# A decoder trunk on one core: value products of two heads at a time, four heads as one run

## The chip, the cores and the metric

One core of a Trainium2 chip runs the whole program. The metric is the device time of one launch in microseconds (us); the figure for a kernel is the median of its runs. The engines are TensorE (PE in the profile; PEld is its loading of weights), VectorE (DVE), ScalarE (ACT), GpSimd (POOL) and SyncE (SP, which here only issues transfers).

## The reference

Two decoder layers over 1024 tokens of width 1024, in fp32. Layer 0, which the change touches, is attention with two families of eight heads of 64 columns each. Layer 1 is a recurrent layer. Each layer ends with a gated embedding. For a block of 128 queries:

```
# NSA heads (2 groups of 4 heads share keys and values)
p_c = softmax(q . compressed keys + bias);   o_c = p_c @ compressed values
imp = per group, sum of p_c over heads and over the blocks that overlap
sel = top 8 of the 64-key blocks by imp (first, current and previous forced)
o_s = softmax(q . k over selected blocks + bias) @ v_s
o_w = softmax(q . k over the last 512 keys + bias) @ v_w
o_a = g0 * o_c + g1 * o_s + g2 * o_w
# DSA heads (all 8 share one key and value head)
sel = top 256 keys by an indexer's score
o_b = softmax(q . k over selected keys + bias) @ v
y = concat(o_a * silu(a_z), o_b * silu(b_z)) @ w_out
```

The compressed keys and values come from windows of 32 tokens (stride 16) through a small two-layer network with a tanh-formed SiLU (`cmp_w1`, `cmp_w2`).

## The kernel before

**Ahead of attention.** Weights are projected one 128-column chunk at a time (`proj`, L197): 48 products of 512 columns, as each operand is split into a high and a low part. Beside the projections VectorE finds, for each query block t of 2 to 7, the threshold of the top 256 keys (`search_step`), and then `choose(t)` (L475) turns scores into a mask `mall`. The last two blocks, 4 and 3, are chosen after the projection that makes the compressed keys' input (L606 to L609). `blocks_of(w, ps)` (L548) then scales the projected keys (w = 0) or values (w = 1) into `kc2`, copies them shifted by one token, and adds the position terms into two tiles `blk`. `compress(w)` (L572) multiplies these by four loaded parts `w1` (products `ps_hid`), and goes over a tanh, a transposition (`ps_hidt`) and a second product (`ps_cmp`). `first_keys` projects the first half of the window and the selected-block keys (`ps_kw`). The scratch tiles `tk`, `kc2`, `blk`, `w1` and others share seven buffers of the pool `big`.

**Attention** (`attention`, L815) goes over 16 blocks: eight query blocks t, each for the two groups p. Each block has 12 heads or units: four window heads, four DSA heads, four selected-block heads, all with the queries on the output partitions of the scores. Unit j passes three stages:

- `scores` (L633): products `ps_s` of up to 512 columns into PSUM, bias or mask and a running minimum on VectorE (L653), exponential with its sum on ScalarE (L657), division and gate on VectorE or GpSimd (L662). The result is `L`, with one row per query.
- four units later `transposed` (L665): TensorE transposes each 128 keys of `L` into the PSUM tile `ps_pt`, ScalarE copies that into `pt`.
- six units later `weighted` (L678), for two units at a time: for each key tile one product for the first head and one for the second, each with 64 columns of values as weights and 128 queries as moving columns. The head's number decides which half of the 128 output partitions of `ps_o` is written.

`begin` (L796) opens the accumulation in `ps_o` with the compressed branch, and `finish` (L802) multiplies it by the gate path into `y`. There is one PSUM bank for `ps_o`, three for `ps_s`, three for `ps_pt` and one (tag "c") for the compressed branch's scores `ps_c` and transposes `ps_ct`. During unit 5 of a block, `prepare` (L756) works out the compressed branch of the next block with `compressed` (L689). `projections` (L823) weaves the second halves of the window and selected keys (`ps_fill`) into the first blocks.

**What sets the order.** A scheduler orders each engine's instructions by data and priority when the program is built; instructions issued through `PV`, `PA` and `PG` (class `Pinned`) keep the order in which the program gives them. On the chip each engine goes through its list in that order and waits where an input isn't there.

Of the kernel before, what the change touches and what calls it, by code (L numbers as in the profile page):

```python
# [25 lines left out]
STEPS = (2, 3)  # L26
WARM = 14
LOAD, PREP = 1, 5
# [30 lines left out]
def trunk_kernel(ctx: ExitStack, tc: tile.TileContext, a, out):  # L59
# [318 lines left out]
    A.activation(biasc[:, :, 48:63], ps[:, :240].rearrange("p (j h) -> p h j", h=16)[:, :8], AF.Copy)  # L378
# [169 lines left out]
    def blocks_of(w, ps):  # L548
        src = []
        for g in range(2):  # L550
            own = slice(g * 64, g * 64 + 64)
            k2 = big(name="kc2")
            V.tensor_tensor(k2[lo], ps[own], nrow[own], OP.mult)
            A.activation(k2[hi, :1023], k2[lo, 1:], AF.Copy)
            src.append(k2)
        for q in range(2):
            bt = big(name="blk")
            b = bt.rearrange("p (l g c) -> p l g c", l=8, g=2)
            V.memset(b[:, :, :, 63:], 0.0)
            for g in range(2):  # L560
                k2 = src[g][:]
                win = bass.AP(tensor=k2.tensor, offset=k2.offset + q * 16, ap=[k2.ap[0], [2, 8], [16, 63]])
                V.tensor_tensor(b[:, :, g, :63], win,
# [69 lines left out]
    def scores(t, g, h, q, keys, k0, far, near, scale, vi):  # L633
# [8 lines left out]
        for c, m in zip(cut, np.diff(cut).tolist()):  # L642
            s = psum.tile([128, 512], F32, name="ps_s", tag="s", bufs=3)
# [21 lines left out]
    def transposed(L, t, k0):  # L665
        nk = t + 1 - k0 // 128
        ps = []
        for b in range(0, nk, 4):
# [7 lines left out]
        return ps  # L676

    def weighted(pair, O, last):  # L678

        nk = len(pair[0][0])  # L680
        for i in range(nk):
            for ps, d in pair:
                h, vi = d["h"], d["vi"]
                c = h // 2 + (2 if vi == 4 else 0)
                T.matmul(O[(h % 2) * 64:(h % 2) * 64 + 64, c * 128:c * 128 + 128],  # L685
                         tok[:, d["k0"] // 128 + i, vi * 64:vi * 64 + 64], ps[i],
                         start=False, stop=last and i == nk - 1, skip_group_check=True)

    def compressed(g, t, q):  # L689
        s = psum.tile([128, 512], F32, name="ps_c", tag="c", bufs=1)  # L690
        for h in range(4):
            for i in range(2):
                T.matmul(s[:, h * 64:(h + 1) * 64], q[:, i, h, :], kcs[:, g * 64:(g + 1) * 64],
                         start=i == 0, stop=i == 1)
# [33 lines left out]
        pt = psum.tile([128, 512], F32, name="ps_ct", tag="c", bufs=1)  # L728
# [4 lines left out]
        return p, sel  # L733
# [22 lines left out]
    def prepare(u):  # L756
# [35 lines left out]
        u.heads = win[:2] + dsa[:2] + win[2:] + dsa[2:] + chosen  # L792
# [3 lines left out]
    def begin(u):  # L796
        u.O = psum.tile([128, 512], F32, name="ps_o", tag="o", bufs=1)
        T.matmul(u.O[:, :256], vc2[:, u.p], u.cmp, start=True, stop=False, skip_group_check=True)
# [16 lines left out]
    def attention():  # L815
# [4 lines left out]
        prepare(blocks[0])  # L820
        units = [(u, k) for u in range(len(order)) for k in range(12)]
# [33 lines left out]
        for j in range(len(units) + AHEAD):  # L855
            for _ in range(FILL[min(j, len(FILL) - 1)]):
                next(fill, None)
            if j < len(units):
# [5 lines left out]
                if k == PREP and i + 1 < len(order):  # L864
                    prepare(blocks[i + 1])
            b = j - AHEAD + MID
            if 0 <= b < len(units):
                i, k = units[b]
                d = blocks[i].heads[k]
                pend[b] = transposed(pend[b], d["t"], d["k0"])  # L870
# [13 lines left out]
    first = attention()  # L884
    leave("ps1", "att", "l0")
# [422 lines left out]
def _layout(i):  # L1308
# [10 lines left out]
    cols = lambda s, n: w[:, s:s + n]  # L1319
    o["wa"] = chunks(np.concatenate([cols(2456, 256), cols(2712, 64), cols(2328, 64), cols(512, 256), cols(768, 128),  # L1320
# [43 lines left out]
```

## Time and profile before

| | us |
|---|---|
| median of 3 runs | 1541.84 (1539.64 to 1543.18) |
| the profiled execution | 1540.62 |
| its span, first to last instruction | 1538.8 |
| attention, first to last `y` | 361.5 (373.6 to 735.1) |
| TensorE busy in the span | 1482.5 |
| VectorE busy | 997.8 |
| ScalarE busy | 799.6 |

The profile is of one execution. Busy time is the union of an engine's instructions, so matmuls that overlap count once, and a matmul's record includes its way through the array after its last column has entered. An idle stretch is put down to what released the engine. The granted clock is given as a share of 2.4 GHz. An fp32 product appears as two records in the trace (1632 records of value products for 816 in the program).

### The profile page before, as it was taken

How to read it: one execution, taken by the hardware profiler on the slowest of the kernel's cores; microseconds unless marked ns; L12 is line 12 of the kernel's file. 1: busy time of each engine (PE TensorE's matmuls, PEld its weight loads, DVE VectorE, ACT ScalarE, POOL GpSimd, SP SyncE). 2: the span in 40 equal slices, each digit the busy share in tenths (PEclk: the TensorE clock that was granted, in tenths of full speed). 3: DMA queues.
4: the chain of work that ended last, by engine and by line, in shares of the span. 5: the costliest groups of instructions: out<-in, count | busy, mean ns of one | idle time of the engine just before them, and what ended most of it. 6: DMA issues, size and time to landing. Idle time of an engine off the chain costs nothing.

```text
span 1538.8 us, 24004 instructions
## 1 busy us (share of the span) xinstructions
PE 1482.5 (96%) x8622; PEld 1223.3 (79%) x8622; DVE 997.8 (65%) x2465; ACT 799.6 (52%) x1667; POOL 509.6 (33%) x506
## 2 busy tenths in 40 slices
PE   9989999987999999999999999999999999999995
PEld 7867887876677888888888889887778888788785
DVE  6378888956789988886234464277776744434446
ACT  6466887225778788777223335366664422223311
POOL 3223443312344443443233412032220123233726
PEclk9999999998999999999999999999999999999997
DMA  4402442354322211200332322011110021222203
GB/s 179 124 28 83 137 138 97 127 176 111 99 69 70 56 49 36 56 22 1 124 103 89 117 76 75 14 49 48 41 40 17 28 83 48 76 85 86 76 1 110
DMA packets 78087, 117.23 MB, mean 76 GB/s; under 512 B 7615, under 2 KB 43072, under 8 KB 77968
## 3 DMA queue, kind: packets, MB, share of 16 engines
q1 hardware_dynamic: 71360, 99.42, 21.1%
q0 software_dynamic: 3952, 12.62, 2.4%
q10 hardware_dynamic: 2656, 3.66, 0.9%
q8 instruction: 68, 1.11, 0.3%
q14 instruction: 51, 0.42, 0.1%
HBM read 94.83 MB, written 24.13 MB: 77 GB/s over the span
## 4 chain that ended last, share of the span: by engine, by line
PE 67%; DVE 15%; ACT 9%; issue 5%; POOL 3%; DMA 2%; SPq 0%; DVEq 0%; POOLq 0%; ACTq 0%
PE ps_proj L194 10%; PE ps_proj L193 10%; PE ps_proj L195 10%; ACT junka L54 5%; PE ps_o L685 5%; PE ps_s L645 5%; PE ps_pt L672 4%; PE ps_gate L193 3%; DVE L L653 3%; PE ps_gate L194 3%; PE ps_gate L195 3%; DVE tk L54 2%; DVE qz L54 1%; DVE junk L54 1%; PE ps_hid L579 1%
## 5 line engine op out<-in xcount | busy, mean ns | idle before, releaser
L121 POOL TENSOR_TENSOR wl<-w,wh 128x512 fp32r<-128x512 f32 (+1 forms) x104 | 152.2, 1482 | 434.7 <-ACT wh L120 434.2
L120 ACT ACTIVATE wh<-w 128x512 fp32r<-128x512 f32 (+1 forms) x104 | 61.1, 621 | 224.3 <-PE ps_proj L194 182.3
L657 ACT ACTIVATE L<-L,st 128x640 f32<-128x640 f32 (+7 forms) x192 | 143.1, 746 | 33.7 <-DVE st L653 26.0
L193 PE MATMUL ps_proj<-x1n,wh 128*128 128x512 f32 x384 | 152.4, 397 | 0.0
L195 PE MATMUL ps_proj<-x1n,wl 128*128 128x512 f32 x384 | 151.8, 395 | 0.0
L194 PE MATMUL ps_proj<-x1n,wh 128*128 128x512 f32 x384 | 151.5, 394 | 0.0
L645 PE MATMUL ps_s<-key,q 128*128 128x256 f32 (+3 forms) x576 | 150.3, 368 | 1.0 <-DVE st L653 0.6
L674 ACT ACTIVATE pt<-ps_pt 128x512 f32<-128x512 f32 (+3 forms) x288 | 124.3, 464 | 37.5 <-PE ps_pt L672 27.5
L193 PE MATMUL ps_proj<-x,wh 128*128 128x512 f32 x336 | 133.1, 396 | 0.4 <-DVE qz L54 0.3
L195 PE MATMUL ps_proj<-x,wl 128*128 128x512 f32 x336 | 133.0, 396 | 0.0
L194 PE MATMUL ps_proj<-x,wh 128*128 128x512 f32 x336 | 132.5, 394 | 0.0
L672 PE MATMUL ps_pt<-cst,L 128*128 128x128 f32 x816 | 125.0, 276 | 5.5 <-DVE L L662 4.3
L685 PE MATMUL ps_o<-pt,tok 128*64 128x128 f32 x1632 | 121.8, 281 | 0.7 <-ACT pt L674 0.7
L54 POOL TENSOR_TENSOR wl<-w,wh 128x512 fp32r<-128x512 f32 x46 | 62.4, 1361 | 169.8 <-ACT wh L54 167.1
L645 PEld LDWEIGHTS ps_s<-key,q 128*128 128x128 f32 x576 | 94.7, 193 | 24.2 <-issue 10.2
L672 PEld LDWEIGHTS ps_pt<-cst,L 128*128 128x128 f32 x816 | 95.2, 141 | 18.6 <-issue 5.5
L685 PEld LDWEIGHTS ps_o<-pt,tok 128*64 128x64 f32 x1632 | 91.7, 137 | 22.5 <-issue 18.4
L54 ACT ACTIVATE junka<-xall,cand 128x384 int8<-128x384 f32 (+2 forms) x93 | 83.6, 899 | 29.2 <-DVE cand L54 27.1
L194 PE MATMUL ps_proj<-y,wh 128*128 128x512 f32 x240 | 93.5, 390 | 0.8 <-DVE y L121 0.8
L193 PE MATMUL ps_proj<-y,wh 128*128 128x512 f32 x240 | 93.5, 390 | 0.1
L195 PE MATMUL ps_proj<-y,wl 128*128 128x512 f32 x240 | 93.4, 389 | 0.0
L54 DVE TENSOR_SCALAR_CACHE_REDUCE junk<-xall,cand 128x512 bf16<-128x512 f32 (+2 forms) x93 | 85.9, 924 | 3.3
(430 smaller groups left out, 3623.7 us busy)
## 6 DMA issues: line engine op xcount, KB each, us to landing
q<-qd SPq DMA_DIRECT2D x64, 256.0 KB, 4.0
w<-in_ra_dram SPq DMA_DIRECT2D x48, 256.0 KB, 2.7
w<-in_wa_dram POOLq DMA_DIRECT2D x46, 256.0 KB, 3.1
qd<-qst SPq DMA_DIRECT2D x32, 256.0 KB, 3.2
w<-in_wo_dram SPq DMA_DIRECT2D x32, 256.0 KB, 2.7
w<-in_gatew_dram SPq DMA_DIRECT2D x32, 256.0 KB, 2.8
x<-in_x_dram SPq DMA_DIRECT2D x8, 512.0 KB, 8.8
zd<-qz SPq DMA_DIRECT2D x8, 512.0 KB, 2.6
```

The costliest lines, as they stand in the source:

```text
L54: return self.tc.keep_in_program_order(getattr(self.eng, name)(*args, **kw))
L120: A.activation(h, src, AF.Copy)
L121: eng.tensor_tensor(l, src, rd(h), op=OP.subtract)
L193: T.matmul(ps, wh, xh, start=first, stop=False)
L194: T.matmul(ps, wh, xl, start=False, stop=False)
L195: T.matmul(ps, wl, xh, start=False, stop=last)
L645: T.matmul(s[:, :m], q[:, i, h, :], keys[:, k0 + c:k0 + c + m], start=i == 0, stop=i == 1)
L653: V.tensor_tensor_reduce(view(L[:, x:y]), view(s[:, x - c:y - c]), pen, 1.0, prev, OP.add, OP.min, st[:, k:k + 1])
L657: A.activation(L[:, :n], L[:, :n], AF.Exp, bias=prev, scale=-1.0, accum_out=st[:, 2:3])
L672: T.transpose(pt[:, i * 128:(i + 1) * 128], L[:, (b + i) * 128:(b + i + 1) * 128], ident)
L674: A.activation(p[:, :m * 128], pt[:, :m * 128], AF.Copy)
L685: T.matmul(O[(h % 2) * 64:(h % 2) * 64 + 64, c * 128:c * 128 + 128], tok[:, d["k0"] // 128 + i, vi * 64:vi * 64 + 64], ps[i], start=False, ...
```

## The change

It does five things:

- `transposed` puts two heads (k and k + 1) into one tile `pt` of 128 x 2 x 512, and `weighted` takes four heads at once: for each key tile two products, each of 64 value columns by 256 moving columns (two heads), the first into the upper half of the output partitions, the second into the lower. They run when the fourth head's turn has come, with a raised priority (`BURST`), and `begin` stands directly ahead of the first of them.
- The twelve heads of a block go in the order window, DSA, selected, four each (before: two window, two DSA, two window, two DSA, four selected). So that heads 0 and 1 lie in one half and 2 and 3 in the other, the compressed branch, the gate columns, the gate paths and the output weights are permuted, on the host or by a bias copy in four pieces.
- The compressed branch's scores use the bank ring of `ps_s`, which has four banks instead of three; its transposes use that of `ps_pt`. Tag "c" is gone.
- `compressed` is cut in two: its transposes (`compressed_rows`) come at unit 10 of the block instead of unit 5.
- `blocks_of` for keys and values comes ahead of the `choose` of block 4 and of block 3, and its VectorE and ScalarE instructions are pinned.

```diff
-    for t in ends[0]:
-        choose(t)
     blocks_of(0, ps)
+    choose(ends[0][0])
     ps = proj(None, X, w=got[17][0])
     wks = prefetch(5)
+    blocks_of(1, ps)
     compress(0)
-    blocks_of(1, ps)
+    choose(ends[0][1])
     first_keys(wkw, kw)
...
-            s = psum.tile([128, 512], F32, name="ps_s", tag="s", bufs=3)
+            s = psum.tile([128, 512], F32, name="ps_s", tag="s", bufs=4)
...
-            p = small.tile([128, 512], F32, name="pt", bufs=PT)
-            A.activation(p[:, :m * 128], pt[:, :m * 128], AF.Copy)
-            ps += [p[:, i * 128:(i + 1) * 128] for i in range(m)]
+            p = first["pt"][b // 4] if j else small.tile([128, 2, 512], F32, name="pt", bufs=PT)
+            A.activation(p[:, j, :m * 128], pt[:, :m * 128], AF.Copy)
+            d["pt"].append(p)
...
-        for i in range(nk):
-            for ps, d in pair:
-                h, vi = d["h"], d["vi"]
-                c = h // 2 + (2 if vi == 4 else 0)
-                T.matmul(O[(h % 2) * 64:(h % 2) * 64 + 64, c * 128:c * 128 + 128],
-                         tok[:, d["k0"] // 128 + i, vi * 64:vi * 64 + 64], ps[i],
-                         start=False, stop=last and i == nk - 1, skip_group_check=True)
+        for i in reversed(range(nk)):
+            for r in (1, 0):
+                T.matmul(O[r * 64:r * 64 + 64, c:c + 256], tok[:, d["k0"] // 128 + i, vi * 64:vi * 64 + 64],
+                         quad[2 * r]["pt"][i // 4][:, :, i % 4 * 128:i % 4 * 128 + 128],
+                         start=False, stop=last and i == 0, skip_group_check=True)
...
-        s = psum.tile([128, 512], F32, name="ps_c", tag="c", bufs=1)
+        s = psum.tile([128, 512], F32, name="ps_c", tag="s", bufs=4)
...
-        pt = psum.tile([128, 512], F32, name="ps_ct", tag="c", bufs=1)
+        return pc, sel
+
+    def compressed_rows(pc):
+        pt = psum.tile([128, 512], F32, name="ps_ct", tag="pt", bufs=3)
...
-        u.heads = win[:2] + dsa[:2] + win[2:] + dsa[2:] + chosen
+        u.heads = win + dsa + chosen
...
-                if k == 0:
-                    begin(u)
-                if k % 2:
-                    weighted([(pend.pop(c - 1), u.heads[k - 1]), (pend.pop(c), u.heads[k])], u.O, k == 11)
+                if k % 4 == 3:
+                    with tc.high_priority(offset=BURST):
+                        if k == 3:
+                            begin(u)
+                        weighted(u.heads[k - 3:k + 1], u.O, k == 11)
```

What this does to the order on TensorE is seen at three places. The first is in the middle of attention, at query block 5, before the change (`ps_s` are scores, `ps_pt` transposes, `ps_o` value products; x10 is ten in a row):

```order
L672 MATMUL ps_pt<-cst,L 128x128 x5
L685 MATMUL ps_o<-pt,tok 64x128 x10
L645 MATMUL ps_s<-key,q 128x384 x2
L645 MATMUL ps_s<-key,q 128x256 x2
L672 MATMUL ps_pt<-cst,L 128x128 x5
L645 MATMUL ps_s<-key,q 128x384 x2
L645 MATMUL ps_s<-key,q 128x256 x2
L672 MATMUL ps_pt<-cst,L 128x128 x5
L685 MATMUL ps_o<-pt,tok 64x128 x10
L645 MATMUL ps_s<-key,q 128x384 x2
```

On the same engine, in the same part of the program, after the change:

```order
L647 MATMUL ps_s<-key,q 128x256 x2
L676 MATMUL ps_pt<-cst,L 128x128 x5
L647 MATMUL ps_s<-key,q 128x384 x2
L647 MATMUL ps_s<-key,q 128x256 x2
L676 MATMUL ps_pt<-cst,L 128x128 x5
L647 MATMUL ps_s<-key,q 128x384 x2
L647 MATMUL ps_s<-key,q 128x256 x2
L676 MATMUL ps_pt<-cst,L 128x128 x4
L688 MATMUL ps_o<-pt,tok 64x256 x10
L676 MATMUL ps_pt<-cst,L 128x128
L647 MATMUL ps_s<-key,q 128x384 x2
L647 MATMUL ps_s<-key,q 128x256 x2
```

A run of value products came after every second head and comes after every fourth, with as many products of twice the width. Over the whole program 123 runs with 816 products became 48 with 408; of the 123, 44 had an odd count.

The second place is on TensorE at the end of the projections, before the change (`ps_proj` is the last projection, `ps_hid` the first compressing product, `ps_kw` the window keys):

```order
L194 MATMUL ps_proj<-x_109,wh 128x512
L195 MATMUL ps_proj<-x_109,wl 128x512
L579 MATMUL ps_hid<-w_2608,blk 128x256 x4
L579 MATMUL ps_hid<-w_2614,blk 128x256 x4
L579 MATMUL ps_hid<-w_2620,blk 128x256 x4
L579 MATMUL ps_hid<-w_2626,blk 128x256 x4
L193 MATMUL ps_kw<-x_102,wh 128x512
```

And on TensorE around the same four groups of `ps_hid` after the change:

```order
L195 MATMUL ps_kw<-x_103,wh 128x512
L196 MATMUL ps_kw<-x_103,wl 128x512
L194 MATMUL ps_kw<-x_103,wh 128x512
L581 MATMUL ps_hid<-w_2615,blk 128x256 x4
L581 MATMUL ps_hid<-w_2621,blk 128x256 x4
L581 MATMUL ps_hid<-w_2627,blk 128x256 x4
L581 MATMUL ps_hid<-w_2633,blk 128x256 x4
L195 MATMUL ps_kw<-x_103,wh 128x512
```

`ps_hid` followed the last projection directly; now 34 products of `ps_kw` stand between (24 of the window keys, 10 of the selected keys). The parts of `w1` lie in other buffers: 2621 and 2627 in those of the second `kc2` pair, 2615 in that of `tk`, and 2633 in that of 2615.

The third place is on TensorE where attention begins, before the change (`ps_fill` are the woven-in key projections, `ps_c` the first compressed scores):

```order
L195 MATMUL ps_kw<-x_105,wl 128x512
L193 MATMUL ps_fill<-x_106,wf 128x512
L194 MATMUL ps_fill<-x_106,wf 128x512
L195 MATMUL ps_fill<-x_106,wf 128x512
L193 MATMUL ps_fill<-x_106,wf 128x512
L194 MATMUL ps_fill<-x_106,wf 128x512
L195 MATMUL ps_fill<-x_106,wf 128x512
L193 MATMUL ps_fill<-x_107,wf 128x512
L194 MATMUL ps_fill<-x_107,wf 128x512
L195 MATMUL ps_fill<-x_107,wf 128x512
L193 MATMUL ps_fill<-x_107,wf 128x512
L194 MATMUL ps_fill<-x_107,wf 128x512
```

On TensorE at the start of attention after the change:

```order
L581 MATMUL ps_hid<-w_2712,blk 128x256 x4
L588 MATMUL ps_hidt<-cst,hid 128x128 x2
L598 MATMUL ps_cmp<-sm,hidt 128x64 x2
L696 MATMUL ps_c<-kcs,q 128x64 x8
L647 MATMUL ps_s<-key,q 128x128 x12
L736 MATMUL ps_ct<-cst,pc 128x128 x2
L804 MATMUL ps_o<-pct,vc_2455 128x256
L194 MATMUL ps_fill<-x_106,wf 128x512
L195 MATMUL ps_fill<-x_106,wf 128x512
L676 MATMUL ps_pt<-cst,L 128x128
```

Twelve products of `ps_fill` stood ahead of `ps_c`; all of them now stand behind the first product into `ps_o`, and no `ps_kw` stands beside the second compression's last steps.

## Rows read from the trace of the kernel before

**Rows 1.** The page: busy us, share of the span and instructions of each engine.

```profile
PE 1482.5 (96%) x8622; PEld 1223.3 (79%) x8622; DVE 997.8 (65%) x2465; ACT 799.6 (52%) x1667; POOL 509.6 (33%) x506
```

**Rows 2.** Busy by stretch: length, PE, PEld, DVE, ACT, POOL (instructions), clock, DMA, GB/s.

```profile
464.40:484.50 20.10, 20.10 (x178) 15.61 (x177) 17.59 (x76) 16.94 (x42) 7.94 (x11) 1.00 0.24 67
484.50:505.90 21.40, 21.03 (x197) 17.69 (x196) 20.16 (x86) 17.83 (x42) 8.87 (x12) 1.00 0.23 64
413.00:709.20 296.20, 289.63 (x2661) 241.23 (x2660) 254.25 (x1013) 235.87 (x566) 123.60 (x166) 1.00 0.19 51
373.60:735.10 361.50, 349.53 (x3143) 288.07 (x3144) 292.13 (x1166) 279.21 (x689) 145.57 (x193) 0.99 0.20 52
```

**Rows 3.** Chain of waits from 373 to 740 us: shares by engine, tile and line.

```profile
by line: PE ps_o L685 19.5%; PE ps_s L645 19.2%; PE ps_pt L672 15.8%; DVE L L653 11.7%; issue 5.5%; ACT L L657 2.1%; DVE L L662 1.8%; POOL pc L727 1.7%; ACT pt L674 1.7%; DVE y L807 1.6%; DVE L L660 1.6%; PE ps_ct L730 1.5%; DVE imp L718 1.
```

**Rows 4.** Waits of VectorE, 350 to 740 us: total us, times, longest.

```profile
DVE L L653 <- PE ps_s L645: 22.8, 33, 2.2
```

**Rows 5.** TensorE in order of time, 542 to 547 us: start, us, instruction, count.

```profile
542.50 0.71 PE L672 MATMUL ps_pt<-cst,L 128*128 128x128 f32 x5
543.14 1.31 PE L685 MATMUL ps_o<-pt,tok 128*64 128x128 f32 x20
...
545.08 0.71 PE L672 MATMUL ps_pt<-cst,L 128*128 128x128 f32 x5
...
546.20 0.71 PE L672 MATMUL ps_pt<-cst,L 128*128 128x128 f32 x5
```

**Rows 6.** TensorE in order of time, 462 to 470 us.

```profile
462.38 0.88 PE L685 MATMUL ps_o<-pt,tok 128*64 128x128 f32 x12
...
465.78 0.60 PE L798 MATMUL ps_o<-pct,vc 128*128 128x256 f32 x2
...
469.56 0.87 PE L685 MATMUL ps_o<-pt,tok 128*64 128x128 f32 x10
```

**Rows 7.** Instructions on `ps_o`: duration ns least/median/most, first and last start.

```profile
L798 PE MATMUL ps_o<-pct,vc x32: 378/379/735, 357.1 to 710.8; 128*128 128x256 f32 x32
```

**Rows 8.** Waits of TensorE, 360 to 740 us.

```profile
PE ps_ct L730 <- POOL pc L727: 4.3, 8, 0.9
...
PE ps_ct L730 <- DVE pc L713: 1.5, 1, 1.5
...
PE ps_o L798 <- DVE y L807: 0.7, 2, 0.4
```

**Rows 9.** TensorE in order of time, 317 to 358 us; in brackets idle before.

```profile
317.29 9.27 PE L579 MATMUL ps_hid<-w,blk 128*128 128x256 f32 x32 [4.83 <-DVE blk L563]
...
333.07 7.07 PE L579 MATMUL ps_hid<-w,blk 128*128 128x256 f32 x32
...
347.36 0.47 PE L193 MATMUL ps_fill<-x,wf 128*128 128x512 f32 x1 [0.88 <-DVE kwp L501]
...
350.23 0.97 PE L693 MATMUL ps_c<-kcs,q 128*128 128x64 f32 x8
...
354.29 0.30 PE L672 MATMUL ps_pt<-cst,L 128*128 128x128 f32 x1 [2.61 <-DVE L L662]
...
357.08 1.16 PE L798 MATMUL ps_o<-pct,vc 128*128 128x256 f32 x2
```

**Rows 10.** Busy by stretch after two waits; the granted clock is third from last.

```profile
317.30:321.40 4.10, 4.10 (x10) 3.29 (x11) 3.32 (x3) 0.87 (x1) 1.02 (x1) 0.50 0.27 100
...
356.20:362.40 6.20, 6.20 (x23) 4.74 (x22) 3.65 (x20) 3.52 (x16) 1.27 (x1) 0.50 0.32 86
```

**Rows 11.** VectorE in order of time, 301 to 319 us.

```profile
301.33 2.47 DVE L54 TENSOR_TENSOR_SCAN tk<-junk,zero 128x640 f32<-128x640 bf16 x1
...
310.90 2.47 DVE L553 TENSOR_TENSOR kc<-ps_proj,nrow 64x1024 f32<-64x1024 f32 x2
...
315.26 3.85 DVE L563 TENSOR_TENSOR blk<-kc,sm 128x504 f32<-128x504 f32 x2
```

**Rows 12.** Transfers issued, 300 to 345 us: count, KB each, us to landing.

```profile
w<-in_w_dram SPq DMA_DIRECT2D x8, 512.0 KB, 3.9
```

More of the change, by code (lines that the diff above doesn't have):

```diff
@@ L26 @@
 STEPS = (2, 3)
+BURST = 2000
 WARM = 14
-LOAD, PREP = 1, 5
+LOAD, PREP, POST = 1, 5, 10
 LB = 5
@@ L377, in trunk_kernel @@
         T.matmul(ps[:, i * 16:(i + 1) * 16], ohb[:, 0, 96 - 16 * c:224 - 16 * c], tbb, start=True, stop=True)
-    A.activation(biasc[:, :, 48:63], ps[:, :240].rearrange("p (j h) -> p h j", h=16)[:, :8], AF.Copy)
+    for j, h in enumerate((0, 2, 1, 3)):
+        A.activation(biasc[:, j:8:4, 48:63], ps[:, :240].rearrange("p (j h) -> p h j", h=16)[:, h:8:4], AF.Copy)
     qi = []
@@ L552, in blocks_of @@
             k2 = big(name="kc2")
-            V.tensor_tensor(k2[lo], ps[own], nrow[own], OP.mult)
-            A.activation(k2[hi, :1023], k2[lo, 1:], AF.Copy)
+            PV.tensor_tensor(k2[lo], ps[own], nrow[own], OP.mult)
+            PA.activation(k2[hi, :1023], k2[lo, 1:], AF.Copy)
             src.append(k2)
@@ L663, in scores, with transposed @@
         return L
-    def transposed(L, t, k0):
-        nk = t + 1 - k0 // 128
-        ps = []
+    def transposed(L, d, first):
+        nk = d["t"] + 1 - d["k0"] // 128
+        j = d["h"] % 2
+        d["pt"] = []
         for b in range(0, nk, 4):
@@ L672, in transposed, with weighted @@
                 T.transpose(pt[:, i * 128:(i + 1) * 128], L[:, (b + i) * 128:(b + i + 1) * 128], ident)
[L673 to L687 removed]
+            p = first["pt"][b // 4] if j else small.tile([128, 2, 512], F32, name="pt", bufs=PT)
+            A.activation(p[:, j, :m * 128], pt[:, :m * 128], AF.Copy)
+            d["pt"].append(p)
+    def weighted(quad, O, last):
+        d = quad[0]
+        vi, c = d["vi"], 256 if d["vi"] == 4 else 0
+        nk = d["t"] + 1 - d["k0"] // 128
+        for i in reversed(range(nk)):
[3 more added lines that the diff above has]
+                         start=False, stop=last and i == 0, skip_group_check=True)
     def compressed(g, t, q):
[L690 to L691 removed]
+        s = psum.tile([128, 512], F32, name="ps_c", tag="s", bufs=4)
+        for j, h in enumerate((0, 2, 1, 3)):
             for i in range(2):
[L693 removed]
+                T.matmul(s[:, j * 64:(j + 1) * 64], q[:, i, h, :], kcs[:, g * 64:(g + 1) * 64],
                          start=i == 0, stop=i == 1)
@@ L797, in begin @@
         u.O = psum.tile([128, 512], F32, name="ps_o", tag="o", bufs=1)
-        T.matmul(u.O[:, :256], vc2[:, u.p], u.cmp, start=True, stop=False, skip_group_check=True)
+        T.matmul(u.O[:, :256], vc2[:, u.p], u.cmpt, start=True, stop=False, skip_group_check=True)
     Y = [{}, {}]
@@ L820, in attention @@
         prepare(blocks[0])
+        blocks[0].cmpt = compressed_rows(blocks[0].cmp)
         units = [(u, k) for u in range(len(order)) for k in range(12)]
@@ L865, in attention @@
                     prepare(blocks[i + 1])
+                if k == POST and i + 1 < len(order):
+                    blocks[i + 1].cmpt = compressed_rows(blocks[i + 1].cmp)
             b = j - AHEAD + MID
@@ L869, in attention @@
                 d = blocks[i].heads[k]
-                pend[b] = transposed(pend[b], d["t"], d["k0"])
+                transposed(pend.pop(b), d, blocks[i].heads[k - k % 2])
             c = j - AHEAD
```

19 lines of the change are left out of this document (12 added, 7 removed).

## The prediction

> **What bounds the kernel now.** I read the page first: TensorE is busy for 96% of the span and VectorE for 65% [rows 1]. The change touches the attention stage, so I then took the busy times between the first and the last output product `y` (373.6 to 735.1 us): TensorE 349.5 of 361.5 us, VectorE 292.1, ScalarE 279.2 [rows 2]. VectorE's share is not the same everywhere: 86% over the middle part (413 to 709 us), 94% in its densest stretch (484 to 506), 58% in the 65.3 us around the middle. The chain of waits over that stage runs through `ps_o`, `ps_s` and `ps_pt`, three TensorE products, for over half of its length [rows 3], and VectorE stands idle for 22.8 us until scores arrive [rows 4]. So TensorE sets the pace there.
>
> A busy TensorE is not yet one that streams columns. The value products come in pairs, two heads on the two halves of the output partitions, whose records overlap: a run of 20 records takes 1.31 us, one of 12 takes 0.88, so a pair of records costs (1.31 - 0.88) / 4 = 0.108 us [rows 5, 6]. What remains is the cost of going into and out of a run. From transposes at 542.50 over a run of ten pairs and the next scores to the transposes at 545.08 are 2.58 us; from there over scores of the same shape (four records) to the transposes at 546.20, with no run between, 1.12 us [rows 5]. The run added 1.46 us, of which ten pairs are 1.08. About 0.37 us is fixed per run, and all of it counts as busy.
>
> The Trainium skill ("Trainium Kernel Development and Optimization", Performance Expectations) calls matmul busy time a bad measure of how close a kernel is to its limit and points to the weight loads' share. The trace agrees: in the middle part TensorE shows 98% and the weight loads 81% [rows 2]. By the busy row alone nothing could be gained in this stage; by the rows above some 30 us can.
>
> **The change, part by part.**
>
> *Fewer runs.* The order has 123 runs of value products before and 48 after (three per block, sixteen blocks). 75 fewer at 0.36 us (0.37 rounded down for runs that end in transposes) are 27 us.
>
> *No unpaired products.* Of the 123 runs 44 have an odd number of products. Ten records take 0.87 us where twelve take 0.88 [rows 6]: the product without a partner costs as much as a pair. 44 x 0.108 = 4.8 us go, since every quad has even counts.
>
> *256 columns.* The one fp32 product with 256 columns in the trace has records 0.60 - 0.38 = 0.22 us apart [rows 6, 7], as much as two of 128 columns (0.216). Half as many products of twice the width stream equally long: nothing either way. Halving the weight loads gives nothing, as they lie beside streaming products.
>
> *Compressed branch.* TensorE waits 4.3 + 1.5 us in front of its transposes `ps_ct` and 0.7 us at the head of a block [rows 8]. They now come five heads later, and the block's first product three heads later, when those inputs should be there. Five of the 6.5 us go if nothing else is late, none if the wait just moves. I take 3. The bank it gave up is the fourth for scores.
>
> Together 27 + 4.8 + 3 = 35 us of TensorE's time in this stage.
>
> *What is late next.* VectorE's work does not shrink. Over the middle 296.2 us it is busy 254.3 [rows 2]. Were its share to rise to the densest stretch's 94%, the stretch would take 270.5 us, 26 less; at 92% 276 (20 less), at 90% 282.5 (14 less), at 88%, as in 464 to 484 us, 289 (7 less). The 65.3 us around it have slack on VectorE; their share of the 75 runs, 65.3 / 361.5, is 14, which with the unpaired products' share makes 6 us. So the stage gains 13 us at 88%, 26 at 92%, 32 at 94%, and 35 at most. I take 25: fuller than the usual stretch, since scores have a bank more, but short of the densest, since TensorE is now away from scores for up to twice as long at a time, and ScalarE too comes to some 85%.
>
> *Key blocks ahead of picks.* Now TensorE waits 4.83 us at the first hidden product `ps_hid`, for blocks that VectorE forms only after both pick passes; then the 32 records take 9.27 us against 7.07 for the second set [rows 9], since after the wait the granted clock is 0.50 (1.2 GHz) for 4 us [rows 10]: 7.0 us lost. The blocks' VectorE work (310.90 to 319.1, with contention) can start at 301.3 instead, where the pick's scan stands [rows 11], beside a projection of 11 us, so the wait should go. But the order puts 34 window and selected-key products ahead of `ps_hid`, and the four parts of its weights now take buffers that are freed late: by the pick's scratch, by the second key blocks' inputs, and by the first part itself. A part lands 3.9 us after its issue [rows 12]. I expect the second part about 3.5 us after TensorE asks. Both pick passes stay on VectorE; the last ends before its mask is read, but the first mask stands ahead of the split of the selected keys' weights on ScalarE: half a us.
>
> So TensorE's list runs as follows, with 2.87 us for twelve key products (347.36 to 350.23 [rows 9]): from 312.5 the 34 products 8.1 us and the half; the first set 7 and its gap 3.5; fourteen more key products and small steps 4.2; the second set 7; and 2.5 us (my allowance; none to 4) for the hidden activation and copies that no key products cover any more. `ps_c` then starts near 345 instead of 350.23, 5 us earlier, and with it the chain to `ps_o` at 357.08. The twelve fill products that lay ahead of `ps_c` are still to be paid behind it: 2.9 us at full clock, twice that at half. Before, TensorE waited 2.61 us in this chain [rows 9] and came out at a granted clock of 0.50 for some 6 us [rows 10]; now it has less to do there, so I expect the same again and charge 4 us. One us is gained. Bounds: 8 gained (no gap for the weights, fills at full clock) and 6 lost (three weight parts late by 3.5 us each against the 4.83 removed).
>
> The rest (POOL and SP order, the four small bias copies at 0.2 us, the permuted weights) lies beside other work, and TensorE's order after the last value product is the same.
>
> **Sum.** 25 + 1 = 26 us off the profiled execution's 1540.62 us: 1514.6. The median of the runs shown, 1541.84, lies 1.2 us above that execution: 1516 us.
>
> **Rivals.**
>
> *VectorE takes over.* If it stays at the 88% that long stretches show, the stage gains 13 us and the start nothing: 1541.8 - 13 = 1529 us. For it: 88% is what VectorE shows in a stretch such as 464 to 484 us in which TensorE is never idle [rows 2], and ScalarE, near 80%, waits on it in turn. Against it: most of its idle time is for TensorE.
>
> *Everything arrives.* All 35 us and the start's 8: 1541.8 - 43 = 1499 us. For it: the 94% stretch; against it: three engines would have to be nearly full at once.
>
> *Pairs no longer overlap (slower).* The two halves overlap only while neighbouring products go to different halves and both have their operand; at a run's start, or without a partner, records follow each other singly. The moving operand is now two pieces 512 elements apart. If no pairs overlapped, 816 pairs x 0.108 = 88 us would be added against 35: 1541.8 + 53 = 1595 us. It decides once two fifths of the pairs are lost. Against it: the halves alternate as before, and the two-piece operand is read in the same number of columns.
>
> *Long runs starve VectorE (no gain).* A quad of eight key tiles holds TensorE for 32 x 0.108 = 3.5 us where a pair held it 1.7. If score banks don't cover that in the 24 runs of query blocks 4 to 7, some 1.4 us each (half a run of five to eight tiles), 34 us come back: about 1541 us. Against it: four banks are two long heads.
>
> That the change doesn't do what it says I exclude by the order.
>
> **How the numbers follow.** Forecast 0.60 (1505 to 1523 us), VectorE as bound 0.20 (1523 to 1536), everything 0.09 (under 1505), starving runs 0.06 (1536 to 1547), lost pairs 0.05. A change under 0.2%, about 3 us, can't be told from none here. Faster: 0.60 + 0.20 + 0.09 = 0.89; same 0.04 and the other 0.02 of the starving runs slower, with the lost pairs 0.07. The range 1500 to 1532 leaves out about 0.06 below and 0.14 above.
>
> **What would show it.** Right: 48 runs, each with about 0.36 us beyond its pairs; 816 records, in pairs 0.22 us apart; the stage from first to last `y` near 336 us with VectorE at 87% over all, over 90% in the middle; no `ps_ct` waits of note; `ps_hid` starting near 321 with a gap for its weights. Wrong: records 0.22 us apart one by one, VectorE still at 86% with TensorE idle for ScalarE, a stage over 348 us, or a first `ps_c` later than 350.

## The result and the profile after

The changed kernel takes 1519.16 us (median of 4 runs, 1516.88 to 1520.03); the kernel before took 1541.43 us beside it. The ratio is 0.9852, interval 0.9838 to 0.9866: 22 us faster. Forecast were 1516 us, between 1500 and 1532. The profiled execution took 1518.43 us, with a span of 1516.6.

The stretch from the first to the last `y` now runs from 377.8 to 714.7 us. Its busy times, columns as in [rows 2], then those of the part from the third `y` to the last but one:

```profile
377.80:714.70 336.90, 323.92 (x2339) 248.16 (x2340) 287.70 (x1166) 271.15 (x689) 145.56 (x193) 1.00 0.21 55
408.10:686.40 278.30, 270.74 (x1964) 207.75 (x1964) 249.67 (x1006) 226.87 (x561) 123.20 (x165) 1.00 0.21 54
```

336.9 us against 361.5 [rows 2], 24.6 less; 25 were forecast. TensorE's busy time fell by 25.6 us (349.53 to 323.92), its idle time in the stretch is 13.0 where it was 12.0. VectorE comes to 85% over all and 90% in the middle (87% and over 90% were forecast).

Two runs of value products, from the trace of the changed kernel in order of time:

```profile
438.89 1.52 PE L688 MATMUL ps_o<-pt,tok 128*64 128x256 f32 x12
...
455.87 1.95 PE L688 MATMUL ps_o<-pt,tok 128*64 128x256 f32 x16
```

Twelve records of 256 columns take 1.52 us, sixteen 1.95: a pair adds 0.43/2 = 0.215 us, as forecast. [rows 6] had 0.88 us for twelve of 128 columns. All 48 runs are unbroken and hold whole pairs. What VectorE waited for (the first line is of the kernel before, 375 to 735 us, so of its stretch alone where [rows 4] has a longer one), and then what TensorE waited for, which answers to [rows 8]:

```profile
DVE L L653 <- PE ps_s L645: 19.6, 30, 2.2
```

```profile
DVE L L655 <- PE ps_pt L676: 6.2, 11, 0.9
DVE L L655 <- PE ps_s L647: 5.0, 14, 1.1
```

```profile
PE ps_o L688 <- ACT pt L678: 4.7, 8, 1.6
PE ps_pt L676 <- ACT pt L678: 3.3, 8, 0.7
...
PE ps_ct L736 <- POOL pc L730: 0.8, 1, 0.8
...
PE ps_ct L736 <- DVE st L660: 0.5, 2, 0.3
```

VectorE's idle time for scores fell from 19.6 to 5.0 us. The waits in front of `ps_ct` have all but gone from this stretch, but as much idle time now stands in front of value products and transposes, for ScalarE's copies `pt`.

Ahead of the stretch the start looks like this (waits of TensorE, 312 to 377 us, then TensorE in order of time), which answers to [rows 9]:

```profile
PE ps_hid L581 <- DMA w<-in_w_dram: 2.8, 1, 2.8
PE ps_ct L736 <- DVE pc L716: 2.6, 1, 2.6
PE ps_c L696 <- DMA q<-qd: 2.4, 1, 2.4
...
PE ps_s L647 <- DMA q<-qd: 0.9, 1, 0.9
```

```profile
350.37 1.68 PE L696 MATMUL ps_c<-kcs,q 128*128 128x64 f32 x8 [2.44 <-DMA q<-qd]
...
354.69 1.09 PE L647 MATMUL ps_s<-key,q 128*128 128x128 f32 x4 [0.89 <-DMA q<-qd]
358.42 0.69 PE L736 MATMUL ps_ct<-cst,pc 128*128 128x128 f32 x2 [2.63 <-DVE pc L716]
```

The wait for the key blocks is gone, and `ps_hid` starts at 322.61 us; its second weight part is 2.8 us late. The first `ps_c` stands at 350.37 us, where it was (350.23); ahead of it TensorE waits 2.4 us for its `q`, which was not foreseen. The first `y` comes 4.2 us later than before. Some 2.4 us of this is no effect of the change: the last projection of the stage ahead ended at 312.5 us in the execution before and at 314.8 in this one, and over the eleven kernels below anywhere from 312.3 to 316.1. Counted from the end of that projection, the first `ps_c` comes 2.3 us earlier than before (35.5 us against 37.8) and the first `y` 1.8 us later (62.9 against 61.1).

### The profile page after: what moved, and what is told of

Read it like the earlier page. It is cut to its first block, busy times and chain, and to the rows that moved or that the text cites. A ratio compares the mean times of both kernels' runs of the same rounds, so it can differ in the third digit from the quotient of the medians.

```text
span 1516.6 us, 22213 instructions
## 1 busy us (share of the span) xinstructions
PE 1456.3 (96%) x7806; PEld 1183.5 (78%) x7806; DVE 992.4 (65%) x2465; ACT 791.4 (52%) x1670; POOL 507.9 (33%) x506
## 4 chain that ended last, share of the span: by engine, by line
PE 68%; DVE 12%; ACT 9%; issue 5%; POOL 3%; DMA 3%; SPq 0%; POOLq 0%; DVEq 0%; ACTq 0%
PE ps_proj L194 12%; PE ps_proj L195 12%; PE ps_proj L196 11%; ACT junka L55 4%; PE ps_o L688 4%; PE ps_pt L676 3%; PE ps_gate L194 3%; PE ps_gate L195 3%; PE ps_gate L196 3%; PE ps_s L647 3%; DVE L L655 3%; ACT L L659 1%; PE ps_v L196 1%; PE ps_v L194 1%; PE ps_v L195 1%
## 5 line engine op out<-in xcount | busy, mean ns | idle before, releaser
L121 ACT ACTIVATE wh<-w 128x512 fp32r<-128x512 f32 (+1 forms) x104 | 61.1, 621 | 223.0 <-PE ps_proj L195 181.7
L647 PE MATMUL ps_s<-key,q 128*128 128x384 f32 (+3 forms) x576 | 148.9, 365 | 2.1 <-DVE st L655 1.0
L688 PE MATMUL ps_o<-pt,tok 128*64 128x256 f32 x816 | 98.7, 385 | 5.1 <-ACT pt L678 4.7
L55 ACT ACTIVATE junka<-xall,cand 128x384 int8<-128x384 f32 (+2 forms) x93 | 83.6, 899 | 29.5 <-DVE cand L55 27.4
L688 PEld LDWEIGHTS ps_o<-pt,tok 128*64 128x64 f32 x816 | 54.4, 136 | 38.8 <-ACT pt L678 14.4
```

The source lines that it names most:

```text
L55: return self.tc.keep_in_program_order(getattr(self.eng, name)(*args, **kw))
L121: A.activation(h, src, AF.Copy)
L647: T.matmul(s[:, :m], q[:, i, h, :], keys[:, k0 + c:k0 + c + m], start=i == 0, stop=i == 1)
L688: T.matmul(O[r * 64:r * 64 + 64, c:c + 256], tok[:, d["k0"] // 128 + i, vi * 64:vi * 64 + 64], quad[2 * r]["pt"][i // 4][:, :, i % 4 * 128 ...
```

## The experiments

Times are medians, beside runs of the kernel before on the same chip (1541.3 to 1541.9 us). "After" is the changed kernel, 1519.16 us.

The granted clock differs between the profiled executions. In after, in the start alone and in q first it is 1.00 (2.4 GHz) from 364 us to the end of attention. In most of the others it falls once more to 0.50 (1.2 GHz), for 7 to 14 us near the block that ends with the second `y`. Here is such a stretch of the kernel with q and w1 early, then the same stretch of after; shortly ahead of both TensorE had waited 1.1 us for a copy `pt`:

```profile
366.10:379.80 13.70, 13.70 (x57) 10.61 (x54) 8.22 (x47) 9.06 (x40) 5.27 (x9) 0.50 0.50 130
374.40:388.10 13.70, 11.83 (x77) 8.89 (x78) 9.89 (x58) 10.81 (x49) 7.16 (x11) 1.00 0.58 161
```

In five of the kernels below that block takes 15.9 to 16.5 us with such a fall, where it takes 13.3 in after and 13.4 in q first. So some 3 us between two profiled executions can be clock. Why it fell in some and not in others, no run shows.

**The start undone.**

```
-            PV.tensor_tensor(k2[lo], ps[own], nrow[own], OP.mult)
-            PA.activation(k2[hi, :1023], k2[lo, 1:], AF.Copy)
+            V.tensor_tensor(k2[lo], ps[own], nrow[own], OP.mult)
+            A.activation(k2[hi, :1023], k2[lo, 1:], AF.Copy)
...
+    for t in ends[0]:
+        choose(t)
     blocks_of(0, ps)
-    choose(ends[0][0])
     ps = proj(None, X, w=got[17][0])
     wks = prefetch(5)
-    blocks_of(1, ps)
     compress(0)
-    choose(ends[0][1])
+    blocks_of(1, ps)
     first_keys(wkw, kw)
```

> The changed kernel with the old start: both pick passes ahead of the key blocks, the blocks not held in written order. The quads stay. Theory (the new start brings the first ps_c some 2 us nearer to the end of the last projection, and loses more behind it, to fill products and a late q load): first y 2 us earlier after the last projection than in the changed kernel, 1517 us. Rival (the new start is worth what its removed wait promised, and the first quads cost the time up to the first y): 1521 us or more.

Measured: 1525.36 us, ratio 0.9893 (0.9878 to 0.9909); 6 us slower than after. The rival's side, but not by its mechanism. What SyncE's queue, then TensorE waited for:

```profile
SPq L189 <- POOL wf L122: 10.9, 1, 10.9
```

```profile
PE ps_hid L581 <- DVE blk L565: 4.9, 1, 4.9
PE ps_c L696 <- DMA q<-qd: 4.7, 1, 4.7
```

With this order the first block's `q` loads stand on SyncE's queue behind a second load of fill weights, whose buffer POOL holds for 10.9 us. So 4.7 us of wait are a new accident of the queue, beside the old 4.9 in front of `ps_hid`. This run doesn't give the price of the start.

**The start alone**: the same lines, put the other way round into the kernel before.

> The kernel before with the new start alone (123 runs of value products, 128 columns). Theory (start loses a little): 1543 us, first y 2 us later after the last projection. Rival (start gains): 1539 us or less. Either way most of the 22 us must be missing.

Measured: 1539.58 us, ratio 0.9992 (0.9983 to 1.0001): 1.7 us less, which can't be told from none; the first `y` comes 2.8 us later behind the last projection (63.9 us against 61.1). Its stage:

```profile
378.40:734.30 355.90, 345.02 (x3132) 284.51 (x3131) 292.55 (x1162) 279.49 (x686) 145.84 (x193) 1.00 0.20 53
```

From this kernel to after are 20.4 us: the quads (value products of four heads as one run), the order of the heads, the compressed branch and the score banks, with the start alike in both.

**Width.** Each product of 256 columns as two of 128, halves alternating:

```
-            for r in (1, 0):
-                T.matmul(O[r * 64:r * 64 + 64, c:c + 256], ..., quad[2 * r]["pt"][i // 4][:, :, ...])
+            for j in (1, 0):
+                for r in (1, 0):
+                    T.matmul(O[r * 64:..., c + j * 128:c + j * 128 + 128], ..., quad[2 * r]["pt"][i // 4][:, j, ...])
```

> The changed kernel with each value product of 256 columns as two of 128, halves alternating; still 48 unbroken runs of whole pairs, 816 products. Theory (a run's cost is in going in and out, columns stream equally long): 1519 us, within 2. Rival (the gain is from half as many instructions and weight loads): most of the 22 us come back, 1535 us or more.

Measured: 1524.57 us, ratio 0.9890 (0.9876 to 0.9903), between the two expectations. Three quarters of the gain stay at 128 columns. A run of the same six key tiles' products in this kernel:

```profile
442.91 1.53 PE L689 MATMUL ps_o<-pt,tok 128*64 128x128 f32 x24
```

24 records of 128 columns take 1.53 us, 12 of 256 took 1.52. The columns stream equally long, as expected. The 5 us lie elsewhere: in the eight stretches between the last nine `y` the two kernels differ by 0.3 us or less but for the first two (1.3 and 0.6), and most of the difference arises ahead of that: 3.7 us up to the second `y`. Of these, 2.6 arise in the block in which this execution falls to half clock and after doesn't:

```profile
375.00:388.70 13.70, 13.70 (x67) 11.58 (x68) 8.36 (x49) 9.01 (x41) 5.30 (x9) 0.50 0.48 126
```

So part of the 5 us is clock. That is not all of it: the fastest execution of this kernel took 1522.27 us at a granted clock of 0.986 over the whole span, and after's profiled one 1518.43 at 0.985. Where these 3 to 4 us come from is open.

**The number of runs.** BURST at 20 in place of 2000; the order then breaks the quads into 121 runs, 68 of them odd:

> The changed kernel, 256 columns and quads, with a smaller priority for the value products (20 in place of 2000), so that the order breaks them up: 121 runs, 68 of them odd. Theory (0.36 us fixed for a run, a product without a partner costs as much as a pair): 73 runs more are 26 us, 68 halves of a pair of 0.43 us another 14.6, together 41 us, of which TensorE's 13 us of waits in the stage can swallow some: 1547 to 1560 us. Rival (the number of runs means little, the gain is from the products' width): 1519 to 1525 us.

Measured: 1551.31 us, ratio 1.0068 (1.0055 to 1.0081), as expected: slower than the kernel before, with about as many runs. Three runs of this kernel, then its stage and the part of it from the third `y` to the last but one:

```profile
460.92 1.51 PE L688 MATMUL ps_o<-pt,tok 128*64 128x256 f32 x10
...
482.25 0.65 PE L688 MATMUL ps_o<-pt,tok 128*64 128x256 f32 x4
483.26 0.65 PE L688 MATMUL ps_o<-pt,tok 128*64 128x256 f32 x2
```

```profile
375.50:746.80 371.30, 361.02 (x2339) 256.10 (x2340) 286.07 (x1166) 272.33 (x687) 148.99 (x193) 0.99 0.19 50
408.90:717.30 308.40, 300.98 (x1976) 213.10 (x1974) 249.55 (x1014) 229.77 (x564) 127.69 (x166) 1.00 0.19 49
```

Ten records take as long as twelve (1.51), two as long as four (0.65): an odd run pays a whole pair, and a pair is now twice as wide. TensorE is busy 37.1 us more than in after over the stage (361.02 against 323.92), but the granted clock is 0.50 here from 374.0 to 384.3 us. From the third `y` to the last but one it is 1.00 in both: TensorE is busy 30.2 us more than in after (300.98 against 270.74), with 62 runs more (98 against 36), of which 56 are odd. 56 x 0.216 = 12.1 of it are the odd runs, the other 18.1 us are 62 runs at 0.29 us. So the number of runs is the main cause, at a lower price than the 0.36 forecast. The 10 us by which this kernel is slower than the kernel before agree with what its odd runs cost more over the whole program: 68 x 0.216 = 14.7 against 4.8. By this sum the other parts of the change, which this kernel has too, bring nothing to speak of without the long runs.

**No overlap.** The two loops of a quad exchanged, one half of the partitions after the other:

```
-        for i in reversed(range(nk)):
-            for r in (1, 0):
+        for r in (1, 0):
+            for i in reversed(range(nk)):
```

> The changed kernel with the two loops of a quad exchanged: all key tiles of one half of the output partitions, then all of the other, so that neighbouring products go to the same half. 408 products, 48 runs, as before. Theory (records overlap only between halves; a product then takes its 0.216 us twice over, so 204 pairs of 0.43 us are paid twice, less one pair per run that still meets its other half): 204 x 0.43 = 88, less up to 48 x 0.2 = 10: 1597 to 1607 us. Rival (products overlap whatever half they write): 1519 us.

Measured: 1563.54 us (two runs), ratio 1.0142 (1.0124 to 1.0160): 44 us more, half of what was expected. Runs of 12 and 16 records in it:

```profile
424.25 2.00 PE L688 MATMUL ps_o<-pt,tok 128*64 128x256 f32 x12
...
460.02 2.86 PE L688 MATMUL ps_o<-pt,tok 128*64 128x256 f32 x16
```

Sixteen records take 2.86 us against 1.95 with the halves alternating, twelve 2.00 against 1.52. One more product on each half adds 0.86 us, twice the 0.43 of a pair, so neighbours on one half don't overlap. But where the halves change, the last two products of the one still overlap the first two of the other: in the trace of a run of 16 the starts of the four records on either side of that place lie in pairs 5 to 57 ns apart, the other records follow each other by 0.21 us and more. My sum granted 0.2 us there. With 0.86 us kept in the 42 runs of two and more key tiles and 0.43 in the six of one, 39 of the 88 us don't come: 49 us, measured 44. The mechanism holds; the expectation, and the forecast's slower rival with it, priced it twice too high. Up to 3 us of the 44 can be clock, which falls to 0.50 here from 373.1 to 386.8 us.

**The compressed branch's transposes early.** POST at 5 in place of 10.

> The changed kernel with the transposes of the compressed branch five heads earlier, right behind its softmax, as in the kernel before. Theory (TensorE's waits in front of ps_ct and at the head of a block, 6.5 us before and 1.5 now, come back and half of them counts): 1521 to 1524 us. Rival (such a wait only moves others): 1519 us.

Measured: 1593.18 us, ratio 1.0339 (1.0323 to 1.0355), 74 us more: a miss. TensorE's waits, then the stage:

```profile
PE ps_ct L736 <- POOL pc L730: 37.6, 8, 5.2
PE ps_ct L736 <- DVE pc L716: 15.9, 6, 4.5
```

```profile
377.70:787.30 409.60, 348.75 (x2330) 272.05 (x2328) 304.91 (x1163) 274.59 (x687) 145.65 (x193) 0.91 0.17 45
```

Counted in the traces, these transposes stand 9 to 11 TensorE records behind the last records of `ps_c` in the last eight blocks, 77 to 86 in the kernel before, 51 to 72 in after. The softmax between them takes some 6 us, so TensorE waits 53.5 us for it (37.6 + 15.9), and its granted clock over the stage falls to 0.91. It is not what the kernel before did, so it doesn't measure the part that was changed; it shows what a transpose that comes too early costs.

**Three banks for scores**, one for the compressed branch's scores:

```
-            s = psum.tile(..., name="ps_s", tag="s", bufs=4)
+            s = psum.tile(..., name="ps_s", tag="s", bufs=3)
-        s = psum.tile(..., name="ps_c", tag="s", bufs=4)
+        s = psum.tile(..., name="ps_c", tag="c", bufs=1)
```

> The changed kernel with three PSUM banks for scores and one for the compressed branch's scores alone, as before. Theory (long runs hold TensorE away from scores for up to 3.6 us, and the fourth bank feeds VectorE meanwhile): VectorE's idle time for scores rises from 5 to over 15 us in the stage, 1524 to 1530 us. Rival (VectorE has slack enough): 1519 us, within 2.

Measured: 1530.07 us, ratio 0.9927 (0.9912 to 0.9942): 11 us more than after, at the upper end. VectorE's waits in the stage:

```profile
DVE L L655 <- PE ps_pt L676: 11.4, 13, 1.9
DVE L L655 <- PE ps_s L647: 10.3, 22, 1.0
```

5.0 us became 10.3 where scores came last (not the expected 15), and 6.2 became 11.4 where TensorE's transposes ahead of them did. From the third `y` to the last but one the granted clock is 1.00, as in after:

```profile
410.10:696.10 286.00, 274.62 (x1970) 208.21 (x1969) 248.78 (x1008) 228.25 (x563) 122.12 (x165) 1.00 0.21 53
```

These are 7.7 us more than in after (278.3): half of it idle time of TensorE (11.4 us against 7.6), half busy time, though the value products stand in the same 48 runs. By the medians the fourth bank is worth half of what the whole change gained. The forecast gave it no term of its own. A fourth bank in the kernel before, without the long runs, was not tried.

**VectorE relieved**: the `tensor_scalar` that divides the top-256 heads' rows left out.

> The changed kernel without the division of the top-256 heads' rows by their sums, so that these heads' output is not normalised: VectorE has some 37 us less to do in the stage. Theory (TensorE sets the pace and stands for only 12 us in this stage, half of them for ScalarE): 1510 to 1517 us. Rival (VectorE has taken over as the limit, so its work comes off the time): 1490 us or less.

Measured: 1519.60 us, ratio 0.9852 (0.9838 to 0.9867): as after, and above both expectations. Its stage, then the part from the second `y` on in this kernel and in after, and TensorE's largest wait there:

```profile
380.00:717.20 337.20, 324.41 (x2339) 250.76 (x2340) 263.84 (x1106) 271.40 (x687) 140.31 (x193) 0.99 0.21 55
```

```profile
396.50:717.20 320.70, 308.58 (x2267) 238.63 (x2268) 254.96 (x1066) 261.42 (x650) 134.03 (x184) 1.00 0.20 52
391.10:714.70 323.60, 312.26 (x2267) 239.34 (x2268) 278.80 (x1122) 261.31 (x651) 139.28 (x184) 1.00 0.20 52
```

```profile
PE ps_o L686 <- ACT pt L676: 6.0, 12, 1.3
```

VectorE is busy for 23.9 us less (263.84 against 287.70; the durations of the 60 instructions left out sum to 36.7, but their records overlap others) and little comes of it. In the block that ends with the second `y` this execution stands at half clock (0.50 from 376.3 to 390.0 us) and takes 3.2 us more than after; from there on, at a granted clock of 1.00 in both, it takes 2.9 us less. So of the 24 us some 3 come off the time, at most: TensorE sets the pace, with VectorE at 85%.

**q first.** One line lays out the attention stage's buffers in another order:

```
     small = enter("att", bufs=2)
+    small.tile([128, 1024], F32, name="L", bufs=LB)
```

> The changed kernel with only the attention stage's buffers laid out in another order (the rows L first), so that the first block's q no longer takes the space of the indexer's scores, which the last pick's mask reads. The q loads then wait for nothing but the w1 loads ahead of them on SP's queue. Theory (the second pick, now behind the hidden products, holds q's space and so makes ps_c late): the 2.4 and 0.9 us of waits for q go, and part of the half clock behind them (8 ps_c records 1.7 us where 1.0 at full clock): 1513 to 1516 us. Rival (something else is as late: the softmax's inputs, the biases, TensorE's own products): 1519 us.

Measured: 1517.08 us, ratio 0.9838 (0.9823 to 0.9853), between the two expectations. SyncE's `q` loads in after, then here (in order of time):

```profile
345.54 1.14 SPq L752 DMA_DIRECT2D q<-qd  x2
```

```profile
337.37 1.14 SPq L753 DMA_DIRECT2D q<-qd  x2
```

They are issued 8 us earlier, and TensorE no longer waits for `q`. So the cause of that wait is shown: `q` took the space of the indexer's scores, which the last pick's mask reads, and the change moved that pick behind the hidden products. The 2.1 us by which the time fell are less than two intervals can tell apart.

**q and w1**: besides, two of the first four weight parts in buffers that the indexer had long freed.

```
+            if w == 0 and q in (1, 2):
+                ... v = rel.tile([128, 2, 256], F32, name="w1r", tag="relu") ...
```

> As the kernel with q first, and the second and third of the first four w1 parts in buffers that the indexer freed long ago, so that the first hidden product's weights don't wait for the key blocks' inputs. Theory (these waits are all that the new start costs): the 2.8 us gap inside the first ps_hid goes as well, 1509 to 1513 us. Rival (TensorE arrives earlier at the next late thing, the second set's w1 parts or the first block's softmax): no more than 1 us below the kernel with q first.

Measured: 1513.42 us, ratio 0.9819 (0.9803 to 0.9834): just above the expected range, the fastest of all, and 5.7 us below after, with intervals that don't touch. The first `ps_c` comes 28.5 us after the last projection (after: 35.5), the first `y` 56.8 (62.9). But 2.8 us are given back in the next block (16.1 us against 13.3), where the granted clock (third from last) is 0.50 from 366.1 to 379.8 us:

```profile
342.90:352.90 10.00, 6.22 (x20) 4.35 (x20) 6.22 (x29) 5.71 (x18) 4.71 (x6) 0.50 1.06 300
...
362.90:372.90 10.00, 8.80 (x47) 6.88 (x45) 7.62 (x39) 7.28 (x33) 2.31 (x6) 0.66 0.40 106
372.90:382.90 10.00, 10.00 (x44) 7.50 (x43) 4.73 (x27) 6.17 (x26) 5.34 (x8) 0.65 0.56 144
```

**Fill products first**: twelve of them around the first `ps_c`, to work through these waits.

```
+        for _ in range(2):
+            next(fill, None)
         prepare(blocks[0])
+        for _ in range(2):
+            next(fill, None)
```

> As the kernel with q and w1 early, and twelve of the fill products around the first ps_c (six ahead of it, six behind), their weights loaded between the q loads. They stand where TensorE now waits (1.1 and 0.5 us for the hidden activations, 2.9 us in front of ps_ct) and comes out at a granted clock of 0.50. Theory (the waits that were removed came back partly as half clock; with work in these waits the clock stays up): granted clock of 0.9 and more over the 60 us behind the last projection, 1505 to 1510 us. Rival (the fill weights are not there yet, or the first scores come later and with them VectorE's work): 1513 us or more.

Measured: 1516.90 us, ratio 0.9847 (0.9831 to 0.9863), 3.5 us slower than without. The rival holds as far as that nothing is gained: TensorE now waits for the fill weights, and the half clock stays. That the fills make it slower is not shown. The two intervals still touch, and 1.7 of the 3.5 us arise in the last block, far from the fills, where the granted clock fell to 0.50 for 3.5 us behind waits of 0.7 and 1.1 us. In the kernel without the fills it stayed at 1.00 in that block, where TensorE waited as long. The longest wait at the start, the first stretch at half clock, and that place:

```profile
PE ps_fill L194 <- ACT wf L121: 1.6, 1, 1.6
```

```profile
342.90:352.90 10.00, 9.55 (x29) 7.73 (x30) 2.22 (x12) 3.89 (x10) 4.87 (x6) 0.51 1.07 291
...
700.80:704.30 3.50, 3.50 (x20) 1.98 (x18) 0.00 (x0) 0.10 (x1) 0.21 (x1) 0.51 0.02 5
```

## Why the prediction was right, and where it was not

*Fewer runs, no unpaired products (27 + 4.8 us).* The cause is shown by the run with 121 runs. The size was too high: TensorE's busy time in the stage fell by 25.6 us, not 31.8, and part of that is clock, which was 0.50 for 6.8 us of the stage before (383.0 to 386.4 and 400.1 to 403.5 us). From the third `y` to the last but one, at a granted clock of 1.00 before and after, it fell by 18.9 us (289.63 [rows 2] to 270.74) with 56 runs fewer (92 to 36), 30 of them odd. Less 30 x 0.108 = 3.2 this is 0.28 us per run, and 0.29 by the other experiment, where the forecast took 0.36 from one place of the trace (its rows give 2.58 - 1.12 - 1.08 = 0.38 there, not 0.37). 75 runs at 0.28 are 21 us, not 27. That odd runs cost a whole pair is shown twice over.

The Trainium skill ("TensorEngine Tiling (Array Packing)", Tiling Modes) says that a change of tiling mode drains TensorE, and that tiles of one mode work in parallel. Both agree with this kernel: going into and out of a run of 128 x 64 products costs 0.28 to 0.29 us, a price that the page doesn't give, and twelve records take 1.52 us with the halves alternating and 2.00 without. That this price is the drain, no run separates.

*256 columns (nothing).* Right for a run, 1.52 against 1.53 us. The kernel with 128 columns is 5 us slower all the same; in the profiled execution 2.6 us of that is a block at half clock, the rest is open.

*Compressed branch (3 us).* Wrong as a gain. The waits at `ps_ct` went from 5.8 us to 1.3, but TensorE is idle in the stage as long as before. The prediction's other end, that the wait just moves, is what happened: it moved to ScalarE's copies. What this part did bring is the fourth bank for scores, 11 us by the run with three, about half of it as idle time of TensorE.

*What is late next (25 of 35 us, for VectorE).* The number was met, 24.6, for the wrong reason, so by luck. I cut TensorE's 35 us to 25 because VectorE would fill up. The run with 24 us less VectorE work is no faster by its median and 2.9 us faster at most by its trace, so VectorE at 85% over all cuts 3 us at most, not 10. The 35 were themselves too high, by the run's price and by the compressed branch. Of the 24.6, moreover, some belong to the start, whose late products and half clock no longer fall into this stretch (355.9 us with the start alone, 361.5 before): with the start alike the part of the quads, the order and the banks is 20.4 us by the medians.

*The start (+1 us).* Right within its uncertainty as a sum, 1.7 us less by the start alone. Its terms were off: the wait of 4.83 us went, and the second weight part came 2.8 us late (3.5 were forecast), but behind the last projection `ps_c` came only 2.3 us earlier and not 5, since `q`, for which TensorE waited 2.4 us, was held by the pick that had been moved. I had counted the picks' work on VectorE and not who waits for the space that they read. Against it, nothing like the 4 us charged for the fill products was lost by the second `y` in the kernel with the start alone: 83.6 us after the last projection, where the kernel before took 86.0. There too, half clock stood at other places in the two executions.

*The sum.* 20.4 and 1.7 us are 22 of the 26 forecast. That the total came so close is in part luck: the 35 us were some 9 too high (6 for the runs, 3 for the compressed branch), and the cut for VectorE, of which the runs show 3 at most, took off 10. By the shown prices 26 us were to be had, against 20.4 measured; where the other 5 are is not shown.

Of the rivals, VectorE as the bound is excluded by its own experiment, lost pairs by the length of the runs. (That records follow each other singly at a run's start, as this rival said, the trace doesn't show: the first two of after's runs start 7 ns apart, like the later pairs.) Starving runs are excluded by VectorE's 5.0 us of idle time for scores; with three banks they cost 11 us, so this rival was right that long runs starve VectorE, and the reason given against it, the fourth bank, is what prevents it. "Everything arrives" fell with the 35 us.

Of the forecast's own signs, those for right came true (48 runs, pairs 0.22 us apart, a stage of 336.9 us, hardly a wait at `ps_ct`, `ps_hid` at 322.6 with a gap), and so, nearly, did two of those for wrong: VectorE at 85% with TensorE idle for ScalarE (8.0 of its 13.0 us), and a first `ps_c` at 350.37.

The Trainium skill ("Trainium Kernel Development and Optimization", Performance Expectations) puts the weight loads' share and MFU (the share of the peak arithmetic rate) in place of matmul busy time. TensorE's busy share says nothing here, as the skill warns: 96% of the span before [rows 1] and after. But the weight loads' share fell in the stage, from 80% (288.07 of 361.5) to 74% (248.16 of 336.9), while the kernel got faster, and it is 83% with 128 columns (284.83 of 342.2), 5 us slower. Where products change their width, that share doesn't rank kernels. MFU does here, but only since the kernels do the same arithmetic, so it follows the time.

## What to carry to other kernels

Where small products that use half of the array stand between full ones, count the runs and the products without a partner, and price both from two runs of different length in the trace: the fixed part counts as busy and shows in no wait. When a step is moved, look not only at its own engine, but at who waits for the memory that it still reads: a buffer laid out on top of it can make a load late that has nothing to do with the change. And test the engine that you take for the next limit by leaving work out on it before you let it cut a forecast. Before two profiled executions are compared, compare their granted clock stretch by stretch: here a block at half clock was worth 3 us.

## What the runs showed of the hardware that was not expected

- An odd product at the end of a run costs a full pair: 10 records of 256 columns 1.51 us, 12 the same; 2 records 0.65 us, 4 the same.
- Where the halves change, two products overlap with two even when the rest of the run doesn't: eight records on one half and then eight on the other take 2.86 us, where sixteen alternating ones take 1.95.
- The granted clock can be low though no wait is long, and need not be the same behind the same wait: in the kernel with q and w1 early it is 0.50 from 342.3 to 355.9 and from 366.1 to 379.8 us, though no wait of TensorE there is longer than 2.9 us. Ahead of the second of these it had waited 1.1 us; behind the same wait it stayed at 1.00 in after.
